# Attention sweep: value products one pair of steps later, key splits ahead of transposes, backward mLSTM in three steps

## The chip, the cores and the metric

The kernel runs on one core of one Trainium2 chip. The metric is the device time of one execution in microseconds (us). The core has five engines with a queue each: PE (matmuls and transposes, into PSUM banks), DVE (element-wise work), ACT (activation functions, casts and copies), POOL (element-wise work in SBUF) and SP, whose queue issues nearly all DMA transfers here. Each queue is worked off in order; engines wait for one another only through semaphores.

## The reference

One encoder layer over 2048 tokens of width 1024, in float32. Two groups of heads read one input projection, and their outputs are joined, projected, and followed by a feed-forward layer:

```python
h = rms_norm(x, g_mix_norm[l])
z = h @ w_in[l]
y_a = mlstm_group(q_m, k_m, v_m, o_m, gates, ...)   # 4 heads, forward + backward scan over chunks of 128
y_b = mla_group(c_q, c_kv, k_pe, cos, sin, ...)     # 4 heads, full softmax attention
x = x + jnp.concatenate([y_a, y_b], axis=-1) @ w_out[l]
h = rms_norm(x, g_ffn_norm[l])
x = x + jnp.square(jax.nn.relu(h @ w_ff1[l])) @ w_ff2[l]
```

In the attention group every block of queries is scored against all 2048 keys (128 + 64 values per key and query), a softmax is taken over the row, and the probabilities are multiplied with the values. In the mLSTM group a state matrix runs over the 16 chunks of 128 tokens in both directions; its gates (a cumulative sum of log-sigmoids and a running maximum) are needed before the first chunk.

## The kernel before

**Split products.** A float32 product is made of three passes: each operand is split into a high part (a cast on ACT, line 53, which rounds) and a low part (the difference, line 54, on DVE or POOL), and `mm3` (lines 69 to 71) adds high times high, low times high and high times low. So whatever comes to PE as a second operand first goes through a cast on ACT and a subtraction on DVE or POOL.

**The stages.** The input projection comes first (up to about 455 us of the trace), then the attention sweep with the mLSTM woven into it (about 455 to 1150 us), then the output projection and the feed-forward layer. From the attention sweep on the order of every queue is written out by hand: an instruction stands in its engine's queue where the program's text emits it.

**The attention sweep.** `attention` runs over 16 blocks `b` (4 heads of 4 blocks of 512 queries). A block has 16 steps `s`: for four groups `a` of 128 queries, four key tiles `j` of 512 keys. The global step is `g = 16 b + s`, and the loop takes the steps in pairs (`g0`, `g0 + 1`). The text of a pair is emitted in this order:

- two scores, five matmuls of 512 columns each, into one of three PSUM banks `ps`; behind each score stands DVE's copy with the row maximum (line 1092), which frees the bank;
- two chunks of value products, `pv`, three matmuls each (L69, L70, L71), which lag the scores by 20 steps. A chunk `(j, k)` reads column `k` of the transposed probabilities `pth` and `ptl` of key tile `j`, and each of them is written by the four transposes `a = 0..3` of that key tile;
- at one pair of a block `out`, DVE's product of the finished `pv` bank with the inverse row sums (line 1157);
- one step of the mLSTM generator (`next(work)`), here called the step in the middle of the pair;
- for each of the two steps: the exponential on ACT (line 1103) of probabilities scored four steps earlier, and `transpose_group`: four PE transposes of 128 columns (L1134) into one of two PSUM banks `ptp`, then cast to `pth` on ACT (line 53) and difference `ptl` on DVE (line 54). The transposes of block `b` come 16 steps behind its scores, the value products 20;
- a second step of the mLSTM generator at the end of the pair;
- then, at certain steps, loads and splits for what is to come: queries of the next block (`load_q`, `split_q`), keys of the next head (`load_k`, `split_k`: two casts on ACT and two differences), values (`load_v`, `split_v`).

Key tiles 1 to 3 of the next head are split in the last two pairs of a head, in steps `u = 4, 5, 6` of the last eight. Their buffers are those of the old head's tiles, which come free as its last scores are read.

**The mLSTM generator** gives up the word at each `yield`, and so decides only at which half pair its instructions stand. `mlstm_prelude` makes the gate tables: a chain of small operations, with PE transposes of `gs` (L662) and of `mr` (L673), between them eight short scans on DVE (L669), then tables `gn`, which the weights `kw` need. `mlstm_steps` then runs backward over chunks 15 to 1 in groups of two: per group one step with the outer products of the weighted keys `kw` and the values (PE, L759, one PSUM bank `pm` of two for each chunk), two steps in which DVE adds them to the running state (L768, L771) and the state is stored and the next values and keys are loaded, POOL weighing the next group's keys (L752) in the first of them, and one step with a load for the forward pass. After that it runs forward over 16 chunks of twelve steps each, whose `finish` has DVE's `num` (L893) and `sgt` (L904).

**The end of the sweep** is written out: after the last pair, the remaining value products of block 14 stand between the transposes of block 15 (`rest(n)` issues `n` chunks from the list `left`).

Of the kernel before, what the change touches and what calls it, by code (L numbers as in the profile page):

```python
# [25 lines left out]
NH = 4  # L26
# [578 lines left out]
def mlstm_prelude(c, psM):  # L605


    nc, tc = c.nc, c.tc
    H = P // 2
    with ExitStack() as st:  # L610
        pool = st.enter_context(tc.tile_pool(name="g_sb", bufs=1, reuse_waits="tile"))

        def bank():
            return psM.tile([P, 512], F32, name="pm")
# [42 lines left out]
        nc.vector.tensor_copy(gs[:, 1:2], cu[:, P - 1:P])  # L657
        yield
        yield
        pr = bank()[0:1, 0:256].rearrange("p (a t) -> p a t", a=2)  # L660
        for j in range(2):
            nc.tensor.transpose(pr[:, j, :], gs[:, j:j + 1], c.ident)  # L662
# [4 lines left out]
        for r in range(8):  # L667
            s = slice(r * NT, (r + 1) * NT - 1)
            nc.vector.tensor_tensor_scan(mr[:, r, 1:], g1[:, 1, s], g1[:, 0, s], 0.0, op0=ALU.max, op1=ALU.add)  # L669
        yield  # L670
        yield
        pm = bank()[:, 0:1]
# [62 lines left out]
def mlstm_steps(c, pool, ps, ld):  # L735


    nc = c.nc
# [176 lines left out]
    def weigh_all(n):  # L915
        for ch in groups[n]:
            kws[ch] = weigh(1, NT - 1 - ch, ld[ch][1])
# [3 lines left out]
    for n, grp in enumerate(groups):  # L921
        outs = [outer(kws.pop(ch), ld.pop(ch)[0]) for ch in grp]
        yield
        for k, ch in enumerate(grp):
            new = back[ch - 1] = advance(1, NT - 1 - ch, outs[k])
            if ch > 4:
                nc.sync.dma_start(c.d_C[ch - 1], new)
                ld[ch - 4] = mlstm_v(c, ch - 4), mlstm_k(c, ch - 4)
            if k == 0 and n + 1 < len(groups):
                weigh_all(n + 1)  # L930
            yield
        if 4 <= n < len(groups):
            loads[n - 4](0)
        yield
    for d in range(2):
        mask(0, d)

# [62 lines left out]
def attention(c, keep, drain, project):  # L1000

    nc, tc = c.nc, c.tc
    with ExitStack() as st:
# [42 lines left out]
        def load_v(h, j):  # L1046
            raw = vraw[h, j] = rp.tile([P, 512], F32, name="raw").rearrange("p (k d) -> p k d", k=4)
            nc.sync.dma_start(raw, c.d_va[j * 512:(j + 1) * 512, h * DV:(h + 1) * DV].rearrange(
                "(k p) d -> p k d", p=P))
# [49 lines left out]
        def softmax(b, a, j):  # L1099
            if (a, j) == (0, 0):  # L1100
                dens[b] = yp.tile([P, 4, 4], F32, name="rd4", bufs=2)
            p = probs[b, a, j]
            nc.scalar.activation(p, p, AF.Exp, bias=maxes[b, a], accum_out=dens[b][:, a, j:j + 1])  # L1103
# [85 lines left out]
        for g0 in range(0, 16 * N, 2):  # L1189
            pair = (g0, g0 + 1)  # L1190
            for g in pair:
                b, s = divmod(g, 16)
                score(b, *divmod(s, 4))
            for g in pair:
                bp, n = divmod(g - 20, 16)
                if bp >= 0:
                    pv(bp, *divmod(n, 4))
                    if n % 4 == 3:
                        next_v(bp, n // 4)
            if g0 % 16 == 2 and g0 > 32:  # L1200
                out(g0 // 16 - 2)()
            for g in pair:
                b, s = divmod(g, 16)
                h, i = divmod(g // 8, 2 * NB)
                u = g % 8
                if g == g0:
                    next(work, None)
                if g > 3:
                    r = g // 4 - 1
                    softmax(r // 4, r % 4, g % 4)  # L1210
                if g >= 16:
                    m = (g - 16) % 16
                    transpose_group(g // 16 - 1, *divmod(m, 4))
                if g > g0:
                    next(work, None)
                if s == 5 and b:
                    invert(b - 1)
                if s == 9 and b:
                    broadcast(b - 1)
                if b < N - 1:  # L1220
                    if s == 1:
                        load_q(*divmod(b + 1, NB))
                    if s == 7:
                        split_q(*divmod(b + 1, NB))
                if h < NH - 1:
                    if i == 2 and u == 1:
                        load_k(h + 1, 0)
                    if i == 4 and u == 1:
                        split_k(h + 1, 0)
                    if i == 6 and u in (4, 5, 6):  # L1230
                        load_k(h + 1, u - 3)
                    if i == 7 and u in (4, 5, 6):
                        split_k(h + 1, u - 3, nc.vector if u == 5 else nc.gpsimd)
                        if u == 6:
                            load_v(h + 1, 0)
                            load_v(h + 1, 1)
                if g in (6, 8, 10, 12):
                    split_v(0, g // 2 - 3)
                    if g < 10:
                        load_v(0, g // 2 - 1)  # L1240
            if g0 == 16 * N - 10:
                after = drain(rp)
                next(after)
        for _ in work:
            pass
        b = N - 1
        left = list(range(12, 16))

        def rest(n):
            for _ in range(n):  # L1250
# [5 lines left out]
        sl.close()  # L1256
        skq.close()
        next(after)
        rest(1)
        transpose_group(b, 0, 1)  # L1260
        softmax(b, 3, 2)
        rest(1)
# [5 lines left out]
        rest(1)  # L1268
        transpose_group(b, 1, 0, True)
        invert(b)  # L1270
        out(b - 1)()
        transpose_group(b, 1, 1)
        transpose_group(b, 1, 2, True)
# [1069 lines left out]
```

## Time and profile before

| | us |
|---|---|
| median of 3 runs (2561.45 to 2563.33) | 2562.35 |
| the profiled execution | 2561.93 |
| its span | 2560.1 |
| PE busy | 2532.7 |
| DVE busy | 1722.4 |
| ACT busy | 1294.7 |
| POOL busy | 376.9 |

Busy time is that of the span. PE's share is 99%, but its matmuls overlap: a matmul of 512 columns is drawn 0.39 us long and the next one starts 0.23 us after it, so busy PE is not PE at its peak, and a short wait may vanish under the drawn end of the matmul before. Waits are given with the engine that ended them; times of single instructions are read from the timeline, in us from the span's start.

### The profile page before, as it was taken

How to read it: one execution, taken by the hardware profiler on the slowest of the kernel's cores; microseconds unless marked ns; L12 is line 12 of the kernel's file. 1: busy time of each engine (PE TensorE's matmuls, PEld its weight loads, DVE VectorE, ACT ScalarE, POOL GpSimd, SP SyncE). 2: the span in 40 equal slices, each digit the busy share in tenths (PEclk: the TensorE clock that was granted, in tenths of full speed). 3: DMA queues.
4: the chain of work that ended last, by engine and by line, in shares of the span. 5: the costliest groups of instructions: out<-in, count | busy, mean ns of one | idle time of the engine just before them, and what ended most of it. 6: DMA issues, size and time to landing. Idle time of an engine off the chain costs nothing. (4 is left out here: it accounts for less than half of the span.)

```text
span 2560.1 us, 35765 instructions
## 1 busy us (share of the span) xinstructions
PE 2532.7 (99%) x12380; PEld 2111.7 (82%) x12380; DVE 1722.4 (67%) x3286; ACT 1294.7 (51%) x2900; POOL 376.9 (15%) x428
## 2 busy tenths in 40 slices
PE   9999999999999999999999999999999999999999
PEld 7888888787888887888888888888888888888887
DVE  5585467666666666678788787977775577666443
ACT  6455444656666676675445554655554323332332
POOL 1211121213223223200100000000000222322000
PEclk9999999999999999999999999999999999999999
DMA  5434234445353453335695555745447644444552
GB/s 176 144 116 144 94 115 143 107 131 112 88 114 109 98 125 95 73 103 189 206 297 191 197 196 191 253 152 167 145 146 278 220 146 147 146 143 145 214 181 95
DMA packets 295930, 392.53 MB, mean 153 GB/s; under 512 B 32261, under 2 KB 176964, under 8 KB 295748
## 3 DMA queue, kind: packets, MB, share of 16 engines
q1 hardware_dynamic: 293284, 385.78, 48.1%
q10 hardware_dynamic: 2464, 4.46, 0.5%
q8 instruction: 97, 1.59, 0.3%
q14 instruction: 85, 0.70, 0.1%
HBM read 258.51 MB, written 131.64 MB: 152 GB/s over the span
## 5 line engine op out<-in xcount | busy, mean ns | idle before, releaser
L69 PE MATMUL pd<-w2h,uh 128*128 128x512 f32 x896 | 348.7, 389 | 0.1
L70 PE MATMUL pd<-w2l,uh 128*128 128x512 f32 x896 | 348.6, 389 | 0.0
L71 PE MATMUL pd<-w2h,ul 128*128 128x512 f32 x896 | 348.5, 389 | 0.0
L54 DVE TENSOR_TENSOR ul<-ur,uh 128x1024 fp32r<-128x1024 f32 x110 | 153.7, 1397 | 252.8 <-ACT uh L53 252.7
L53 ACT CAST uh<-ur 128x1024 fp32r<-128x1024 f32 x110 | 116.0, 1055 | 395.5 <-PE pd L70 381.7
L54 DVE TENSOR_TENSOR ptl<-ptp,pth 128x512 fp32r<-128x512 f32 x248 | 171.2, 691 | 202.7 <-ACT pth L53 197.6
L53 ACT CAST pth<-ptp 128x512 fp32r<-128x512 f32 x248 | 143.6, 579 | 163.8 <-PE ptp L1134 162.9
L2011 DVE TENSOR_TENSOR e<-pu,e 128x512 f32<-128x512 f32 x224 | 151.3, 689 | 88.7 <-PE pu L71 87.7
L69 PEld LDWEIGHTS pd<-w2h,uh 128*128 128x128 f32 x896 | 168.2, 188 | 35.5 <-DVE e L2011 0.5
L71 PEld LDWEIGHTS pd<-w2h,ul 128*128 128x128 f32 x896 | 168.2, 188 | 34.9
L70 PEld LDWEIGHTS pd<-w2l,uh 128*128 128x128 f32 x896 | 168.2, 188 | 34.9
L1103 ACT ACTIVATE p<-p,nm 128x512 f32<-128x512 f32 x256 | 185.7, 725 | 0.0
L1092 DVE TENSOR_SCALAR_CACHE_REDUCE p<-ps 128x512 f32<-128x512 f32 x256 | 167.6, 682 | 20.4 <-PE ps L1091 20.3
L2175 POOL TENSOR_TENSOR r<-wr,r 128x512 f32<-128x512 f32 x48 | 78.0, 1624 | 623.9 <-DMA wr<-in_w 573.0
L69 PE MATMUL pz<-wh,hh 128*128 128x512 f32 (+1 forms) x384 | 149.7, 391 | 2.1 <-ACT hh L53 0.8
L71 PE MATMUL pz<-wh,hl 128*128 128x512 f32 (+1 forms) x384 | 150.1, 391 | 0.0
L70 PE MATMUL pz<-wl,hh 128*128 128x512 f32 (+1 forms) x384 | 149.2, 389 | 0.1
L2014 ACT ACTIVATE e<-e 128x512 f32<-128x512 f32 x128 | 80.9, 632 | 121.3 <-DVE e L2011 114.7
L1134 PE MATMUL ptp<-ident,p 128*128 128x128 f32 x992 | 130.3, 273 | 0.3 <-DVE ptl L54 0.3
L1134 PEld LDWEIGHTS ptp<-ident,p 128*128 128x128 f32 x992 | 113.9, 140 | 13.5 <-issue 1.4
L1087 PE MATMUL ps<-kh,qh 128*128 128x512 f32 x256 | 113.0, 441 | 1.7 <-ACT kh L53 1.1
L1879 ACT CAST r<-w1raw 128x512 fp32r<-128x512 f32 x104 | 64.5, 622 | 92.9 <-PE pu L71 92.2
(526 smaller groups left out, 6460.9 us busy)
## 6 DMA issues: line engine op xcount, KB each, us to landing
d_u<-e SPq DMA_DIRECT2D x224, 256.0 KB
ur<-d_u SPq DMA_DIRECT2D x110, 512.0 KB
wr<-in_w SPq DMA_DIRECT2D x96, 256.0 KB
w1raw<-in_w SPq DMA_DIRECT2D x42, 512.0 KB
raw<-in_w_in SPq DMA_DIRECT2D x48, 256.0 KB
r<-in_w SPq DMA_DIRECT2D x22, 512.0 KB
mb<-d_M SPq DMA_DIRECT2D x32, 256.0 KB
acc<-d_x SPq DMA_DIRECT2D x16, 512.0 KB
```

The lines of the kernel that those rows point to most:

```text
L53: r = nc.scalar.copy(hi, src)
L54: (eng or nc.vector).tensor_tensor(lo, src, hi.bitcast(F32), op=ALU.subtract)
L69: nc.tensor.matmul(out, ah, bh, start=first, stop=False, skip_group_check=more)
L70: nc.tensor.matmul(out, ah, bl, start=False, stop=False, skip_group_check=more)
L71: nc.tensor.matmul(out, al, bh, start=False, stop=last, skip_group_check=more)
L1087: nc.tensor.matmul(o, qh[:, qs], kh, start=True, stop=False)
L1092: nc.vector.tensor_scalar(p, o, SCALE, None, op0=ALU.mult, op1=ALU.max, accum_out=maxes[b, a][:, j:j + 1])
L1103: nc.scalar.activation(p, p, AF.Exp, bias=maxes[b, a], accum_out=dens[b][:, a, j:j + 1])
L1134: nc.tensor.transpose(pt[:, k, :], p[:, k * P:(k + 1) * P], c.ident)
L2011: nc.vector.tensor_tensor(out, o, t, op=ALU.add)
L2014: nc.scalar.activation(t, t, AF.Relu)
L2175: nc.gpsimd.tensor_tensor(R, wr, R, op=ALU.subtract)
```

## The change

No arithmetic changes, and each engine has the same instructions in another order. There are five parts, and the end of the sweep is adapted to the first.

- **Value products** lag the scores by 22 steps in place of 20, one pair more; `out` moves with them by a pair. At the end six chunks of block 14 are left in place of four: `rest(2)` stands first, and one more `rest(1)` ahead of `out`.
- **Key splits** of tiles 1 to 3 of the next head stand ahead of the transposes of their step, not behind them, and the tiles that are subtracted on POOL, DVE and POOL are now on POOL, POOL and DVE.
- **Query split** of the second block: at step 11 of the first block in place of 7 (the others stay).
- **Gate chain**: four more yields, two ahead of the transposes of `gs` and two ahead of the transposes of `mr`, so two half pairs each.
- **Backward chunks**: a group of two takes three steps in place of four; the load for the forward pass goes into the last of them. Over eight groups eight steps fall away, so that, with the four that the gate chain takes, the forward pass starts four half pairs earlier.

```diff
@@ mlstm_prelude
         nc.vector.tensor_copy(gs[:, 1:2], cu[:, P - 1:P])
         yield
         yield
+        yield
+        yield
         pr = bank()[0:1, 0:256].rearrange("p (a t) -> p a t", a=2)
...
+        yield
+        yield
         yield
         yield
         pm = bank()[:, 0:1]
@@ mlstm_steps, backward
             if k == 0 and n + 1 < len(groups):
                 weigh_all(n + 1)
+            if ch == grp[-1] and n >= 4:
+                loads[n - 4](0)
             yield
-        if 4 <= n < len(groups):
-            loads[n - 4](0)
-        yield
@@ attention, the loop over pairs
             for g in pair:
-                bp, n = divmod(g - 20, 16)
+                bp, n = divmod(g - 22, 16)
...
-            if g0 % 16 == 2 and g0 > 32:
+            if g0 % 16 == 4 and g0 > 32:
                 out(g0 // 16 - 2)()
...
                     softmax(r // 4, r % 4, g % 4)
+                if h < NH - 1 and i == 7 and u in (4, 5, 6):
+                    split_k(h + 1, u - 3, nc.vector if u == 6 else nc.gpsimd)
+                    if u == 6:
+                        load_v(h + 1, 0)
+                        load_v(h + 1, 1)
                 if g >= 16:
...
-                    if s == 7:
+                    if s == (7 if b else 11):
                         split_q(*divmod(b + 1, NB))
...
-                if i == 7 and u in (4, 5, 6):
-                    split_k(h + 1, u - 3, nc.vector if u == 5 else nc.gpsimd)
-                    if u == 6:
-                        load_v(h + 1, 0)
-                        load_v(h + 1, 1)
@@ attention, the end
-        left = list(range(12, 16))
+        left = list(range(10, 16))
...
-        rest(1)
+        rest(2)
         transpose_group(b, 0, 1)
...
         invert(b)
+        rest(1)
         out(b - 1)()
```

Where the order of the queues moves is shown at three places. Line numbers of the changed kernel are higher by three or four in these parts (L1134 is L1137 there, L759 is L763, L771 is L775, L1092 is L1095).

PE, at the end of the sweep, behind the last scores. `ptp` are the last transposes of block 14, `pm` the first of block 15, L69 to L71 the value products of block 14. Before:

```order
L1134 MATMUL ptp<-ident,p 128x128 x8
L1134 MATMUL pm<-ident,p 128x128 x4
L69 MATMUL pv<-pth,vh 128x512
L70 MATMUL pv<-ptl,vh 128x512
L71 MATMUL pv<-pth,vl 128x512
L1134 MATMUL ptp<-ident,p 128x128 x4
```

And now:

```order
L1137 MATMUL ptp<-ident,p 128x128 x8
L1137 MATMUL pm<-ident,p 128x128 x4
L69 MATMUL pv<-pth,vh 128x512
L70 MATMUL pv<-ptl,vh 128x512
L71 MATMUL pv<-pth,vl 128x512
L69 MATMUL pv<-pth,vh 128x512
L70 MATMUL pv<-ptl,vh 128x512
L71 MATMUL pv<-pth,vl 128x512
L1137 MATMUL ptp<-ident,p 128x128 x4
```

The value products stand one pair later against scores and transposes all through the sweep; here it is seen in two chunks more behind the last transposes. The first of them belong to key tile 2, whose transposes are two pairs back, where before they belonged to tile 3, transposed just ahead.

ACT, in the last two pairs of the first head. L1103 (now L1106) is the exponential, `pth` the cast of a transposed group, `kh` and `rh` the casts of one key tile of the next head, `num` a copy of the mLSTM. Before:

```order
L1103 ACTIVATE p,rd_6347<-p,nm 128x512
L53 CAST pth<-ptp 128x4x128
L53 CAST kh<-raw 128x512
L53 CAST rh<-raw 128x512
L1103 ACTIVATE p,rd_6347<-p,nm 128x512
L53 CAST pth<-ptp 128x4x128
L874 COPY num_6581<-pm 128x258
L53 CAST kh<-raw 128x512
L53 CAST rh<-raw 128x512
```

And now:

```order
L1106 ACTIVATE p,rd_6362<-p,nm 128x512
L53 CAST kh<-raw 128x512
L53 CAST rh<-raw 128x512
L53 CAST pth<-ptp 128x4x128
L1106 ACTIVATE p,rd_6362<-p,nm 128x512
L53 CAST kh<-raw 128x512
L53 CAST rh<-raw 128x512
L53 CAST pth<-ptp 128x4x128
```

The two casts of a key tile moved from behind the cast of the transposes to ahead of it, so each `pth` of these steps has two casts more in front of it.

DVE, in the backward chunks. L771 (now L775) adds an outer product to the state `C`, which frees its PSUM bank; L1092 (now L1095) are the copies of the two scores of a pair, `ptl` the differences of its two transposed groups. Before:

```order
L771 SCALAR_TENSOR_TENSOR C_5717<-C_5636,decb,pm 128x129 x2
L54 TENSOR_TENSOR ptl<-ptp,pth 128x4x128 x2
L771 SCALAR_TENSOR_TENSOR C_5743<-C_5717,decb,pm 128x129 x2
L1092 TENSOR_SCALAR p,mx<-ps 128x512 x2
L54 TENSOR_TENSOR ptl<-ptp,pth 128x4x128 x2
L1092 TENSOR_SCALAR p,mx<-ps 128x512 x2
L1096 TENSOR_REDUCE nm<-mx 128x1
L1157 TENSOR_TENSOR y<-pv,rb 128x512
L771 SCALAR_TENSOR_TENSOR C_5840<-C_5743,decb,pm 128x129 x2
```

And now:

```order
L775 SCALAR_TENSOR_TENSOR C_5768<-C_5711,decb,pm 128x129 x2
L1095 TENSOR_SCALAR p,mx<-ps 128x512 x2
L1099 TENSOR_REDUCE nm<-mx 128x1
L775 SCALAR_TENSOR_TENSOR C_5815<-C_5768,decb,pm 128x129 x2
L54 TENSOR_TENSOR ptl<-ptp,pth 128x4x128 x2
L1095 TENSOR_SCALAR p,mx<-ps 128x512 x2
L1160 TENSOR_TENSOR y<-pv,rb 128x512
L775 SCALAR_TENSOR_TENSOR C_5873<-C_5815,decb,pm 128x129 x2
```

The two additions of a group were followed by nearly a whole pair of other work (copies and differences); now those of the next group follow one half pair sooner. The outer products on PE stood at the end of every second pair; now they stand by turns at the end of a pair and in the middle of the next but one.

## The prediction

> **What bounds the kernel now.** I read the page's first part, then the waits of PE in the attention sweep, then the timeline around the longest of them.
>
> ```profile
> span 2560.1 us, 35765 instructions
> PE 2532.7 (99%) x12380; PEld 2111.7 (82%) x12380; DVE 1722.4 (67%) x3286; ACT 1294.7 (51%) x2900; POOL 376.9 (15%) x428
> ...
> PE pv L69 <- ACT pth L53: 4.8, 7, 1.0
> PE pv L70 <- DVE ptl L54: 3.4, 14, 0.4
> PE pm L673 <- DVE mr L669: 1.8, 1, 1.8
> PE ps L1087 <- ACT kh L53: 1.1, 1, 1.1
> PE pm L759 <- POOL kw L752: 0.8, 1, 0.8
> PE ps L1087 <- DVE p L1092: 0.7, 1, 0.7
> PE ptp L1134 <- DVE ptl L54: 0.3, 1, 0.3
> ```
>
> PE sets the time from end to end. An edit that adds no work and only moves it can win no more than what PE loses in waits, and the rows (waited-for engine, then us in total, times, longest) are all that it loses in the sweep but for 0.2 us: 12.9 us. Each part of the change is aimed at one or two of these rows. The listed figures are too small, though, since a wait is counted from the drawn end of the matmul before. One place shows by how much:
>
> ```profile
> 626.98 0.40 PE L1091 MATMUL ps<-rl,qr 128*128 128x512 f32 x1
> 628.21 0.50 PE L69 MATMUL pv<-pth,vh 128*128 128x512 f32 x1 [0.83 <-ACT pth L53]
> 628.93 0.50 PE L70 MATMUL pv<-ptl,vh 128*128 128x512 f32 x1 [0.23 <-DVE ptl L54]
> 629.27 0.39 PE L71 MATMUL pv<-pth,vl 128*128 128x512 f32 x1
> 629.50 0.39 PE L69 MATMUL pv<-pth,vh 128*128 128x512 f32 x1
> ```
>
> Undisturbed, matmuls start 0.23 us apart (629.27 to 629.50). From 626.98 to 629.27 are three intervals, 0.69 us, and it took 2.29: 1.60 lost, of which 1.06 is listed. Per L69 wait that is 1.23 - 0.23 - 0.83 = 0.17 unlisted; per L70 wait, from 628.21 to 629.27, 1.06 - 0.46 - 0.23 = 0.37.
>
> **The change part by part.**
>
> *Value products a pair later.* They wait because the fourth group of transposes that they read was transposed just ahead of the two scores in front of them. Now a whole pair more lies between, 16 matmuls of 512 columns at 0.23 us and 8 transposes, so 3.7 us and more against a longest lost time of 1.6. All 21 listed waits should go: 4.8 + 3.4 + 7 x 0.17 + 14 x 0.37 = **14.6 us**. The one in the tail (L69 behind the last transposes) is included; the two chunks that are moved into the tail, 6 x 0.23 = 1.4 us, fill that wait. Nothing is queued differently for the buffers: the cast that overwrites an old `pth` comes behind transposes that PE issues after the last products of it; the `pv` bank is freed by `out`, which moved along. I cost these at nothing, because PE's own order covers them.
>
> *Gate chain.* Between the transposes of `gs` and of `mr` stood ten score matmuls, 2.3 us; now twenty, 4.6 us, and eight transposes. The wait was not alone:
>
> ```profile
> 474.95 0.40 PE L1091 MATMUL ps<-rl,qr 128*128 128x512 f32 x1
> 477.10 0.19 PE L673 MATMUL pm<-ident,mr 1*128 1x1 f32 x1 [1.75 <-DVE mr L669]
> 477.83 0.63 PE L1089 MATMUL ps<-kh,ql 128*128 128x512 f32 x1
> 481.19 0.39 PE L1087 MATMUL ps<-kh,qh 128*128 128x512 f32 x1
> ...
> 474.60:477.90 3.30, 1.55 (x8) 0.95 (x7) 3.30 (x11) 3.30 (x9) 2.85 (x3) 0.97 0.00 0
> 477.90:481.40 3.50, 3.50 (x10) 2.75 (x9) 0.96 (x5) 3.03 (x9) 1.62 (x2) 0.54 0.00 0
> 481.40:484.80 3.40, 3.40 (x21) 2.93 (x20) 2.82 (x11) 1.83 (x7) 0.00 (x0) 1.00 0.03 3
> ```
>
> In the stage rows PE was busy 1.55 of 3.30 us, and in the next 3.5 us the granted clock (third figure from the end) was 0.54, then 1.00 again. Eight matmuls from 477.83 to 481.19 took 3.36 us, not 1.84: 1.5 lost. With the wait's 1.8 that is 3.3. The scans don't get shorter, however; they hold DVE, and so its copies of the scores:
>
> ```profile
> 474.02 0.40 DVE L665 COPY g<-pm 1x256 f32<-1x256 f32 x1
> 474.40 0.17 DVE L666 MEMSET mr<- 1x128 f32 x1
> 474.60 2.35 DVE L669 TENSOR_TENSOR_SCAN mr<-g 1x15 f32<-1x15 f32 x8
> 476.88 0.66 DVE L1092 TENSOR_SCALAR_CACHE_REDUCE p<-ps 128x512 f32<-128x512 f32 x1
> ```
>
> PE may run three banks ahead, three scores of 5 x 0.23 us = 3.5. Against that stand 0.40 + 0.17 ahead of the scans, 2.35 and 0.66 for the next copy = 3.6, and what the copy before them is late: I estimate 0.5 us of wait on `ps` in its place. Net **2.8**. The 0.7 on L1087 <- DVE earlier in the chain is untouched.
>
> By the Trainium skill (TensorE: Matmul & The Clock Gate, Part 1: The HAM clock gate) the clock halves after an idle window of about 3.4 us, for which 1.75 us of idleness is too short. The trace shows the half clock right behind a stretch that was idle for half of 3.3 us, so I take it to go with the wait; what follows otherwise is a rival below.
>
> *Backward chunks and `kw`.* The first outer product waited for POOL, which was busy with the query split; four half pairs later it is done with that. 0.8, and 0.17 unlisted as for an L69 wait, = **1.0**. Eight steps fewer cost and win nothing themselves, as PE has the same work in the sweep.
>
> *Key splits.* The wait on `kh` goes (1.1 and again 0.17 = **1.3**), since the casts are one transposed group sooner; the price is that transposes' casts come later. **0.3** on `ptp` I count with it.
>
> Gross: 14.6 + 2.8 + 1.0 + 1.3 + 0.3 = 20.0.
>
> *What comes back.* A wait of PE was also the time in which ACT and DVE caught up. Behind 628.2:
>
> ```profile
> 628.79 0.68 DVE L856 TENSOR_TENSOR mb<-pm,mb 128x512 f32<-128x512 f32 x1
> 629.39 2.68 DVE L893 SCALAR_TENSOR_TENSOR num<-num,rd,num 128x128 f32<-128x128 f32 x4
> 631.99 0.68 DVE L1092 TENSOR_SCALAR_CACHE_REDUCE p<-ps 128x512 f32<-128x512 f32 x1
> ...
> 632.77 0.48 PE L1087 MATMUL ps<-kh,qh 128*128 128x512 f32 x1
> ...
> 1125.14 1.13 DVE L893 SCALAR_TENSOR_TENSOR num<-num,rd,num 128x128 f32<-128x128 f32 x4
> ```
>
> Without 1.6 us of wait PE begins its next score at 631.2 and the second at 632.4, whose bank DVE frees at 632.7: 0.3 of 1.6 returns. The bounds are nothing (all waits end in slack) and the whole 14.6 (each moves to `ps` or `ptp`); I take a tenth, **1.5**, as this place is the nearest row. L893 took 2.68 us while POOL split the queries, 1.13 when POOL was idle. The Trainium skill (SBUF — State Buffer, SBUF: two separate sides) calls the port that the two share an exclusive lock, and the change sets two key splits in a row on POOL; this is one way to the first rival.
>
> At the three head changes each `pth` has casts of 0.62 us in front, two per split:
>
> ```profile
> 952.18 0.62 ACT L53 CAST kh<-raw 128x512 fp32r<-128x512 f32 x1
> 952.70 0.62 ACT L53 CAST rh<-raw 128x512 fp32r<-128x512 f32 x1
> ```
>
> 1.2 to 2.5 us of delay per pair against the 3.7 us that scores and products give before the next transposes need the bank; bounds 0 and 2.5 at each of three, I take 0.7: **2.1**. For the outer products in mid pair I add **0.3**.
>
> Net 20.0 - 3.9 = 16.1. The profiled execution took 2561.93 us (1.8 more than its span, which no part touches), so 2545.8; the median of the runs lies 0.4 above it: **2546.2 us**.
>
> **The rivals.**
>
> *The waits move.* ACT and DVE stay as late as they were and PE meets them at the `ptp` and `ps` banks. If half of the 14.6 returns, half of the three small terms (2.6) too, and the head changes cost 1.1 each, the gain is 7.3 + 2.8 + 1.3 - 3.3 = 8.1: 2554. For it: DVE's 2.68. Against: in the longest stretch
>
> ```profile
> 585.00:1010.00 425.00, 416.75 (x2374) 349.35 (x2373) 278.57 (x709) 291.91 (x831) 131.20 (x135) 1.00 0.43 107
> ```
>
> DVE works 66% and ACT 69% of the time, so each makes up about 1.5 us in a pair of 4.6 (10.3 us for two, with 1.1 of outer products, in the rows of the last rival).
>
> *The clock drop isn't the wait's.* By that page's rule the half rate has another cause, falls on the same stretch of matmuls, and 1.5 us stay: 2547.7. Against it: the one low stretch of the sweep stands right behind its longest wait.
>
> *Nothing moves.* The engines that feed PE set the pace: at 66 and 69% unlikely; then 2561.
>
> *Slower, at the backward groups.* They begin 10.3 us apart, two pairs, and shall begin one and a half apart, 7.7 us:
>
> ```profile
> 514.18 1.10 PE L759 MATMUL pm<-v,kw 128*64 128x129 f32 x16
> 524.50 1.10 PE L759 MATMUL pm<-v,kw 128*64 128x129 f32 x16
> ...
> 514.80 0.57 SPq L731 DMA_DIRECT2D knat<-d_k  x1
> ...
> 518.00 0.62 POOL L752 TENSOR_TENSOR kw<-knat,gn 128x256 f32<-128x256 f32 x1 [2.38 <-DMA knat<-d_k]
> ```
>
> If store, loads and weighing set that distance, PE waits 2.6 us in each of seven groups, longer than the wait that went with the half clock, so 1.5 more each: 7 x 4.1 = 28.7 against 16.1, 2575. It decides once keys are weighed later than the outer products want them. They were loaded at 514.80, weighed by 518.62 and wanted at 524.50, 5.9 us later; 2.6 of that go, and 3.3 remain.
>
> **How the numbers follow.** Forecast 61%, the waits move 17%, the clock rule 10%, nothing moves 8%, slower 4%. The forecast's own bounds are no return (20.0: 2542.4) and all returns doubled (2550); the first rival ends at 2554. The range 2541 to 2555 leaves out the last two cases. About 0.2%, 5 us, is what a measurement of this kernel can tell from no change: faster 0.88, same 0.08, slower 0.04.
>
> **What would show it.** In the changed kernel the waits of `pv` are gone from PE's list, and `ps` and `ptp` rows, if they grow, hold less than 4 us. The transposes of `mr` follow without a wait, and no stage of the sweep is granted half the clock. The forecast is wrong if `ptp` or `ps` waits on ACT and DVE sum to 8 us or more, or if L763 waits for `kw` or the state.

## The result, and the profile after

The changed kernel took 2544.25 us (median of four runs, 2542.08 to 2544.83) against 2562.84 for the kernel before beside it: a ratio of 0.9926 with a 95% interval of 0.9909 to 0.9943. Its profiled execution took 2542.08 us, 19.9 less than that of before. The forecast was 2546.2 us, range 2541 to 2555.

The page's first part in the changed kernel, where PE is busy 9.0 us less than before and its span 19.8 us shorter:

```profile
span 2540.3 us, 35812 instructions
PE 2523.7 (99%) x12380; PEld 2111.3 (83%) x12380; DVE 1726.1 (68%) x3286; ACT 1293.7 (51%) x2900; POOL 380.7 (15%) x428
```

The whole list of PE's waits between 455 and 1140 us there (engine, waited-for line, then us in total, times, longest):

```profile
PE ps L1090 <- DVE p L1095: 2.4, 4, 1.3
PE ptp L1137 <- DVE ptl L54: 0.3, 1, 0.3
PE ps L1155 <- ACT pth L53: 0.2, 1, 0.2
```

The rows on `pv`, `kh`, `mr` and `kw` are gone. What is left on `ps` has one large part, which was not there before; it stands in the gate chain, as PE's timeline shows:

```profile
478.22 0.50 PE L1093 MATMUL ps<-rh,qr 128*128 128x512 f32 x1
478.56 0.40 PE L1094 MATMUL ps<-rl,qr 128*128 128x512 f32 x1
480.30 0.50 PE L1090 MATMUL ps<-kh,qh 128*128 128x512 f32 x1 [1.34 <-DVE p L1095]
...
482.53 0.22 PE L677 MATMUL pm<-ident,mr 1*128 1x1 f32 x1
```

From 478.56 to 480.30 are 1.74 us where 0.23 would do: 1.5 lost. The transposes of `mr` (482.53) follow without a wait, and the stretches that held the half clock before now have the full one (third figure from the end):

```profile
474.60:477.90 3.30, 3.30 (x17) 2.52 (x15) 2.94 (x10) 3.30 (x10) 3.22 (x3) 1.00 0.69 170
477.90:481.40 3.50, 2.08 (x9) 1.23 (x8) 3.40 (x11) 1.61 (x5) 1.55 (x2) 1.00 0.00 0
```

Where did the time come from? One program's stages can be measured by the starts of PE's matmuls. From the last one of the input projection to the first of the output projection, in the timelines of before and after:

```profile
457.77 0.39 PE L71 MATMUL pz<-wh,hl 128*128 128x512 f32 x1
1156.58 0.47 PE L69 MATMUL po<-B11h,r 128*128 128x512 f32 x1
```

```profile
457.74 0.39 PE L71 MATMUL pz<-wh,hl 128*128 128x512 f32 x1
1138.10 0.48 PE L69 MATMUL po<-B11h,r 128*128 128x512 f32 x1
```

That stretch, here called *the sweep*, shrank from 698.8 to 680.4 us, by 18.4; the other 1.4 us fell in the output projection and the first part of the feed-forward layer (0.62 and 0.76), which no part touches. In the profiles of all kernels below, the last matmul of the input projection, the same code in each, started between 457.2 and 460.0 us. So parts of one or two us are compared by the length of the sweep, and even that differed by 0.8 us between two profiles of the changed kernel (680.4, and 681.2 in the last experiment).

Each ratio is to the kernel before that ran beside it, whose median lay between 2562.38 and 2563.71 us.

| kernel | median us | ratio to before, 95% | sweep us |
|---|---|---|---|
| before | 2562.84 | | 698.8 |
| value products alone | 2546.42 | 0.9936, 0.9921 to 0.9951 | 683.8 |
| gate chain alone | 2560.56 | 0.9991, 0.9981 to 1.0 | 695.9 |
| key splits alone | 2562.13 | 0.9998, 0.9988 to 1.0007 | 698.2 |
| backward chunks alone | 2564.22 | 1.0005, 0.9995 to 1.0014 | 700.9 |
| the change | 2544.25 | 0.9926, 0.9909 to 0.9943 | 680.4 |
| the change without key splits | 2544.32 | 0.9929, 0.9917 to 0.9942 | 680.0 |
| the change without backward chunks | 2545.39 | 0.9932, 0.9918 to 0.9946 | 681.6 |
| the change, query split at 7 | 2544.56 | 0.993, 0.9917 to 0.9942 | 680.5 |
| that, scans in halves | 2545.26 | 0.9932, 0.992 to 0.9945 | 681.6 |
| the change, POOL relieved | 2544.88 | 0.9931, 0.9917 to 0.9944 | 680.2 |
| that, loads ahead | 2542.85 | 0.9923, 0.9909 to 0.9936 | 679.0 |
| that, query split at 9 | 2542.19 | 0.9923, 0.991 to 0.9937 | 677.9 |
| the change again, beside the last | 2545.12 | 0.9931, 0.9919 to 0.9944 | 681.2 |

### The profile page after: what moved, and what is told of

Read it like the earlier page. It is cut to its first block, busy times and chain, and to the rows that moved or that the text cites. A ratio compares the mean times of both kernels' runs of the same rounds, so it can differ in the third digit from the quotient of the medians.

```text
span 2540.3 us, 35812 instructions
## 1 busy us (share of the span) xinstructions
PE 2523.7 (99%) x12380; PEld 2111.3 (83%) x12380; DVE 1726.1 (68%) x3286; ACT 1293.7 (51%) x2900; POOL 380.7 (15%) x428
## 5 line engine op out<-in xcount | busy, mean ns | idle before, releaser
L69 PE MATMUL pd<-w2h,uh 128*128 128x512 f32 x896 | 348.8, 389 | 0.1
L71 PE MATMUL pd<-w2h,ul 128*128 128x512 f32 x896 | 348.7, 389 | 0.0
L69 PEld LDWEIGHTS pd<-w2h,uh 128*128 128x128 f32 x896 | 168.2, 188 | 35.4 <-DVE e L2015 0.5
L71 PEld LDWEIGHTS pd<-w2h,ul 128*128 128x128 f32 x896 | 168.2, 188 | 34.9
L1106 ACT ACTIVATE p<-p,nm 128x512 f32<-128x512 f32 x256 | 185.8, 726 | 2.6 <-DVE nm L1099 2.6
L1095 DVE TENSOR_SCALAR_CACHE_REDUCE p<-ps 128x512 f32<-128x512 f32 x256 | 167.4, 682 | 15.2 <-PE ps L1094 15.1
L69 PE MATMUL pz<-wh,hh 128*128 128x512 f32 (+1 forms) x384 | 149.5, 391 | 1.7 <-ACT vo L495 0.7
L71 PE MATMUL pz<-wh,hl 128*128 128x512 f32 (+1 forms) x384 | 150.0, 391 | 0.0
L1137 PE MATMUL ptp<-ident,p 128*128 128x128 f32 x992 | 130.6, 274 | 0.5 <-DVE ptl L54 0.3
L1137 PEld LDWEIGHTS ptp<-ident,p 128*128 128x128 f32 x992 | 113.6, 140 | 14.1 <-issue 1.4
L1090 PE MATMUL ps<-kh,qh 128*128 128x512 f32 x256 | 112.8, 441 | 2.4 <-DVE p L1095 2.4
```

The source lines that it names most:

```text
L69: nc.tensor.matmul(out, ah, bh, start=first, stop=False, skip_group_check=more)
L71: nc.tensor.matmul(out, al, bh, start=False, stop=last, skip_group_check=more)
L1090: nc.tensor.matmul(o, qh[:, qs], kh, start=True, stop=False)
L1095: nc.vector.tensor_scalar(p, o, SCALE, None, op0=ALU.mult, op1=ALU.max, accum_out=maxes[b, a][:, j:j + 1])
L1137: nc.tensor.transpose(pt[:, k, :], p[:, k * P:(k + 1) * P], c.ident)
```

## The experiments

**Each part alone.** The theory: each part removes its own wait, and the value products bring nearly all. The rival: the waits move to `ps` and `ptp`.

*Value products alone* (labels of the kernel before, L1087 for L1090 and so on):

```diff
-                bp, n = divmod(g - 20, 16)
+                bp, n = divmod(g - 22, 16)
...
-            if g0 % 16 == 2 and g0 > 32:
+            if g0 % 16 == 4 and g0 > 32:
...
-        left = list(range(12, 16))
+        left = list(range(10, 16))
```

> The kernel before with only the value products (and out, and the end of the sweep) one pair later. My theory: all waits of pv on pth and ptl go, about 1.5 us come back on ps or ptp, the waits on mr (1.8, with the half clock), kh (1.1) and kw (0.8) stay as they were: 13 us less, 2549 +- 1.5. The rival (waits move): at least half comes back on ps and ptp unless the key splits and the gate chain are changed too, 2555 or more. A second rival (the parts only work together): under 4 us gained.

Measured: 2546.42 us, better than expected. Its list of PE's waits, without the last two rows (0.3 and 0.2):

```profile
PE pm L673 <- DVE mr L669: 2.4, 1, 2.4
PE ps L1087 <- ACT kh L53: 1.0, 1, 1.0
PE ps L1087 <- DVE p L1092: 0.8, 1, 0.8
PE pm L759 <- POOL kw L752: 0.8, 1, 0.8
...
```

All 21 waits of `pv` are gone and no row grew in their place but that on `mr`. Behind the first transposes of the sweep the stage is 15.8 us shorter (673.1 to 657.3), while the first block, from the input projection to the first transposes, lost 0.8 to the longer wait on `mr`. So the rival fell here: in the list nothing of this term returned.

*Gate chain alone* (the four yields; the query split stays at 7):

```diff
         yield
         yield
+        yield
+        yield
         pr = bank()[0:1, 0:256].rearrange("p (a t) -> p a t", a=2)
...
             nc.vector.tensor_tensor_scan(mr[:, r, 1:], ...)
+        yield
+        yield
```

> The kernel before with only the four yields in the gate chain (the query split stays at step 7). My theory: the wait on mr goes and the half clock with it, the scans take 2.35 us as before (in the changed kernel they took 3.45) and leave about 0.5 us of wait on ps, kw has no wait: 3.8 us less, 2558.8 +- 1.5, where the later mLSTM may shift pv waits by 1. If the clock drop isn't the wait's: half clock in the same stretch, 2560.3.

Measured: 2560.56 us, outside the 2558.8 +- 1.5 that was expected and near the 2560.3 of the rival. The rival's half clock isn't there, though: no wait on `mr`, no half clock, 0.56 us on `ps` behind the scans, and the first block is 3.2 us shorter (25.7 to 22.5). That difference is rough. Up to the first transposes the kernel before and those with value products, key splits and backward chunks alone have the same order of work, and took 25.7, 26.5, 26.6 and 23.8 us there, the last without a half clock. Behind the first block the kernel is 0.3 us longer, although the wait on `kw` (0.8) is gone: the forward chunks now end four half pairs later, among the written-out end of the sweep, and the list shows what that costs:

```profile
PE ps L1156 <- ACT pth L53: 0.9, 1, 0.9
PE pm L1138 <- DVE ptl L54: 0.7, 1, 0.7
```

*Key splits alone* and *backward chunks alone*:

```diff
+                if h < NH - 1 and i == 7 and u in (4, 5, 6):
+                    split_k(h + 1, u - 3, nc.vector if u == 6 else nc.gpsimd)
...
-                    if i == 7 and u in (4, 5, 6):
-                        split_k(h + 1, u - 3, nc.vector if u == 5 else nc.gpsimd)
```

> The kernel before with only the key splits (and the value loads behind them) ahead of the transposes, on POOL, POOL, DVE. My theory: the 1.1 us wait on kh goes, but the casts of pth behind it are later and pv still reads them right away, so the pv waits at the three head changes grow by up to 1.2 each: between 1.3 less and 2.3 more, 2562.9 +- 1.5. The rival, that this part wins for itself: 2561 or less with no larger pv wait.

```diff
+            if ch == grp[-1] and n >= 4:
+                loads[n - 4](0)
             yield
-        if 4 <= n < len(groups):
-            loads[n - 4](0)
-        yield
```

> The kernel before with only the backward chunks in three steps (the forward pass eight half pairs earlier). My theory: no time is won or lost, 2562.4 +- 1.5; outer products wait only once, for the first kw (0.8). The rival (loads or the state set the distance of the groups): waits of L759 on kw or C of 2.6 us in seven groups and half clock behind them, up to 2591.

In the whole time neither won anything that could be told from the spread. With the keys first, the wait on `kh` goes, and at that head change the casts in front of `pth` make one value product, still one pair early, wait 1.9 us; all waits on `pth` are 6.3 us (4.8 before), those on `ptl` 2.7 (3.4 before):

```profile
PE pv L69 <- ACT pth L53: 6.3, 6, 1.9
PE pv L70 <- DVE ptl L54: 2.7, 12, 0.3
PE pm L673 <- DVE mr L669: 2.6, 1, 2.6
```

The sweep of this kernel is 0.6 us shorter than before: 0.9 longer in the first block, which this part doesn't touch, and 1.5 shorter behind it. By that the part was worth a little by itself, where the rows on the value products alone would say that it lost.

With the backward chunks alone the slower rival's mechanism shows itself, once, against the expectation that only the first `kw` is waited for. PE's row, and POOL's beside it:

```profile
549.54 1.13 PE L759 MATMUL pm<-v,kw 128*64 128x129 f32 x8 [2.80 <-POOL kw L752]
...
548.87 0.62 POOL L752 TENSOR_TENSOR kw<-knat,gn 128x256 f32<-128x256 f32 x1 [8.59 <-DMA knat<-d_k]
```

The keys came late, the outer product waited 2.8 us for them, and half the clock followed at once. The sweep is 2.1 us longer than before: 4.0 longer behind the first block, and 1.9 shorter in it, where a wait of 2.4 us on `mr` cost no half clock this time.

**One part taken back.**

*Without the key part*:

```diff
-                if h < NH - 1 and i == 7 and u in (4, 5, 6):
-                    split_k(h + 1, u - 3, nc.vector if u == 6 else nc.gpsimd)
...
+                    if i == 7 and u in (4, 5, 6):
+                        split_k(h + 1, u - 3, nc.vector if u == 5 else nc.gpsimd)
```

> The changed kernel without its key part: the splits of the next head's tiles 1 to 3 stand behind the transposes again. Theory: that part is worth nothing by itself once the value products are later: the wait on kh comes back (1.0 to 1.3 us), the small waits on ps and ptp at the three head changes (0.4 + 0.8 + 0.3 us) go, so within 0.5 us of the changed kernel (2542.1 profiled). Rival, the prediction's own sum: the kh wait of 1.3 us comes back and 2.1 us of casts ahead of the transposes go, 0.8 us faster. Other rival: the casts behind the transposes now meet the products of a pair later, pv waits come back at the head changes, 2 us slower.

Measured: sweep 680.0, no difference. By the distances of matmul starts the wait on `kh` at the second head change costs 1.2 us here; in the change the second and third head changes cost 0.39, 0.30, 0.49 and 0.32, together 1.5, on `ps` and `ptp`, and these are gone here. The part exchanges one for the other.

*Without the backward part*:

```diff
-            if ch == grp[-1] and n >= 4:
-                loads[n - 4](0)
             yield
+        if 4 <= n < len(groups):
+            loads[n - 4](0)
+        yield
```

> The changed kernel without its backward part: groups of two chunks in four steps again. Theory: the three steps pay only for the four yields of the gate chain; without them the forward chunks end four half pairs later than in the kernel before and run into the end of the sweep, where PE then waits on casts and differences as in the kernel with the gate chain alone (1.1 + 0.7 us there), so 1.5 to 2 us slower than the changed kernel, 2543.6 to 2544.1 profiled; the keys are weighed with over 2 us of slack. Rival: the groups' closer distance costs PE something that its list of waits doesn't show, and with four steps the time is the same or less.

Measured: sweep 681.6, with 1.2 us on `ptl` and 0.8 on `pth` listed in the tail. Against the first profile of the change that is 1.2 us more, against the second 0.4. The waits are those expected; that the time is longer can't be told from the spread.

*Query split back at step 7*:

```diff
-                    if s == (7 if b else 11):
+                    if s == 7:
```

> The changed kernel with one part undone: the query split of the second block back at step 7. My theory: the eight scans took 3.45 us in place of 2.35 because the two differences of the query split ran on POOL beside them, and that is why the wait on ps in the gate chain was 1.5 us and not the 0.5 that I predicted. Then here the scans take about 2.35 us, the wait is about 0.5 us, and the profiled execution is about 1.0 us below that of the changed kernel (2542.1), so 2541.0. Rival: the scans are long for another reason (the transposes and copies of more steps between): scans 3.45 us, wait 1.5 us, no change in time. Second rival: the split at 7 delays something else in the first block (the weighing of keys on POOL, or a score's copy), and a wait of 0.8 us or more takes the place.

This theory fell. The scans took 3.10 us and the wait on `ps` stayed at 1.5, sweep 680.5. POOL was busy beside the scans all the same, now with the first head's values:

```profile
478.51 3.10 DVE L671 TENSOR_TENSOR_SCAN mr<-g 1x15 f32<-1x15 f32 x8
...
477.45 1.29 POOL L1077 TENSOR_TENSOR qr<-raw,qr 64x512 fp32r<-64x512 f32 x1
478.82 2.67 POOL L54 TENSOR_TENSOR vl<-raw,vh 128x512 fp32r<-128x512 f32 x2
```

*Scans in halves*:

```diff
         for r in range(8):
             ...
-        yield
-        yield
-        yield
-        yield
+            if r in (3, 7):
+                yield
+                yield
...
-                    if s == (7 if b else 11):
+                    if s == 7:
```

> The changed kernel with the query split back at step 7 and the eight scans emitted in two halves of four, each with two of the four yields behind it, so that a score's copy can stand between them on DVE. Theory: the wait on ps comes from DVE held by the scans for longer than three banks cover; halves of 1.2 us leave none, so the whole 1.5 us of wait in the chain goes and the profiled execution is 2540.6. Rival: DVE is late by its sum of work and not by the block of scans; then the wait stays between 0.3 and 0.5 us and nothing is won over the kernel with only the split moved.

The wait on `ps` behind the scans went, but PE then met ACT, which had worked without a pause: 0.84 and 0.69 us were lost at the next transposes, as much as was won, and 0.95 at the outer products. (PE's list names the difference `ptl` on DVE there; DVE itself had waited 2.14 us for ACT's cast `pth`.) Here "the waits move" was true. DVE's two halves say more:

```profile
477.77 1.67 DVE L671 TENSOR_TENSOR_SCAN mr<-g 1x15 f32<-1x15 f32 x4
...
481.19 0.42 DVE L671 TENSOR_TENSOR_SCAN mr<-g 1x15 f32<-1x15 f32 x4
```

Four scans of the same shape take 1.67 us beside a POOL that is busy (478.10 to 481.05, one pause of 0.36) and 0.42 while it is idle (481.05 to 481.69). In the change, three operations of POOL lie beside the eight scans:

```profile
475.50 1.30 POOL L54 TENSOR_TENSOR ql<-raw,qh 128x512 fp32r<-128x512 f32 x1
476.87 1.30 POOL L1077 TENSOR_TENSOR qr<-raw,qr 64x512 fp32r<-64x512 f32 x1
478.25 1.28 POOL L54 TENSOR_TENSOR vl<-raw,vh 128x512 fp32r<-128x512 f32 x1
...
476.20 3.45 DVE L671 TENSOR_TENSOR_SCAN mr<-g 1x15 f32<-1x15 f32 x8
```

**POOL kept out of the way.** The new theory: an operation of DVE that reads SBUF twice and meets one of POOL waits until that one is over.

```diff
+        load_q(0, 1)
         load_v(0, 0)
...
-                    if s == 1:
+                    if s == 1 and b:
                         load_q(*divmod(b + 1, NB))
-                    if s == (7 if b else 11):
+                    if s == 7:
...
-                if g in (6, 8, 10, 12):
-                    split_v(0, g // 2 - 3)
-                    if g < 10:
-                        load_v(0, g // 2 - 1)
+                if g in (18, 22, 26, 30):
+                    split_v(0, (g - 18) // 4)
+                    if g < 26:
+                        load_v(0, (g - 10) // 4)
```

> The changed kernel with POOL and ACT relieved while the gate chain runs: the queries of the second block are loaded ahead of the sweep and split at step 7, and the values of the first head are split at steps 18, 22, 26, 30 in place of 6, 8, 10, 12. Theory: an operation of DVE that reads two SBUF tiles and meets one of POOL waits for the whole of it. With POOL idle the eight scans take 0.9 to 1.2 us in place of 3.45, and f (L650, 1.27 us beside a value split) about 0.3; so both waits on ps in the chain go, 0.85 + 1.51 us. As ACT has five casts less there and doesn't wait for the queries' load, it isn't late at the transposes behind, and the first block and the sweep together take 2.3 us less than the changed kernel's 680.4. Rival one: ACT stays late and PE meets it at ptp, as with the scans in halves: 680.4 to 681.3. Rival two: the keys of a backward group come no sooner while PE does, and about 1 us is lost at the outer products (L763 <- kw): 679.0. If the scans still take 3 us, the theory of the port is wrong.

The scans took 0.76 us, less even than the 0.9 to 1.2 expected, and `f` 0.29, and there was no wait behind them. But the query split now met two other operations of the chain, earlier:

```profile
471.62 1.02 DVE L654 TENSOR_TENSOR u<-li,b 128x128 f32<-128x128 f32 x1
472.68 1.46 DVE L655 TENSOR_TENSOR_SCAN cu<-u 128x128 f32<-128x128 f32 x1
...
471.21 1.29 POOL L54 TENSOR_TENSOR ql<-raw,qh 128x512 fp32r<-128x512 f32 x1 [15.84 <-ACT qh L53]
472.58 1.28 POOL L1077 TENSOR_TENSOR qr<-raw,qr 64x512 fp32r<-64x512 f32 x1
```

`ql` ends at 472.50 and `u` at 472.64; `qr` ends at 473.86 and `cu` at 474.14. Elsewhere these two take 0.29 and 0.43 us. So 1.76 us of DVE went, a wait on `ps` of 1.44 stood there, and the sweep was 680.2: the time was the rival's, by a mechanism that only the theory had.

*The loads ahead*, on top of it:

```diff
+            if ch > 4:
+                kn = mlstm_k(c, ch - 4)
+                ld[ch - 4] = mlstm_v(c, ch - 4), kn
             new = back[ch - 1] = advance(1, NT - 1 - ch, outs[k])
             if ch > 4:
                 nc.sync.dma_start(c.d_C[ch - 1], new)
-                ld[ch - 4] = mlstm_v(c, ch - 4), mlstm_k(c, ch - 4)
```

> The kernel with POOL and ACT relieved, and in the backward groups the loads of the next values and keys stand ahead of DVE's additions and of the store of the state, keys first. Theory: what decides the outer products' wait is when the keys are loaded; with the loads about 1 us sooner the wait on kw is gone, and first block and sweep together take 678.0 us (about 1 us less than without it, if that kernel waits there; the same if it doesn't). Rival: the keys take 6 to 9 us to land whenever they are issued, since the transfers ahead of them in the queue set it; then the wait stays as it is.

The keys for the outer products at 549.6 were weighed by 547.08, and no wait on `kw` is left (0.2 us listed without this part). The sweep is 679.0, where 678.0 was expected. Of the 1.2 us less than without this part, 0.5 lie behind the first block, where the loads stand; the other 0.8 lie in the first block, which it doesn't touch.

```profile
546.46 0.62 POOL L756 TENSOR_TENSOR kw<-knat,gn 128x256 f32<-128x256 f32 x1 [0.44 <-DMA knat<-d_k]
```

*Query split at step 9*, on top of both, and *the change again* on the same chip:

```diff
-                    if s == 7:
+                    if s == (7 if b else 9):
```

> The kernel with POOL and ACT relieved and the loads ahead, and its query split at step 9 in place of 7. At 7 the two differences on POOL met u (L654, 0.29 us alone, 1.02 there) and the scan behind it (L655, 0.42 alone, 1.46 there), which cost a wait on ps of 1.25 us. Theory of the port: POOL's 2.6 us fit between those operations of the gate chain and the eight scans, where DVE only copies scores; u takes 0.29, the scan 0.42, the eight scans 0.8, and no wait on ps over 0.4 us is left in the chain. First block and sweep together 677.7 us, 2.7 below the changed kernel's 680.4. Rival: the split meets the eight scans, or the casts of the queries make ACT late, and 1 us or more of wait on ps or ptp stays: 678.7 or more.

> The changed kernel itself, on the same chip as the quiet one, so that the two are compared directly: 680.4 us for first block and sweep together as in its first profile, with 0.3 us of spread; the median 2 to 3 us above the quiet one's if the waits of the gate chain are what differs, and no more than 1 us if they come back elsewhere.

Now POOL's two operations lie where DVE copies scores out of PSUM, and every operation of the chain has its short time:

```profile
471.54 0.29 DVE L654 TENSOR_TENSOR u<-li,b 128x128 f32<-128x128 f32 x1
471.87 0.43 DVE L655 TENSOR_TENSOR_SCAN cu<-u 128x128 f32<-128x128 f32 x1
...
476.02 0.76 DVE L671 TENSOR_TENSOR_SCAN mr<-g 1x15 f32<-1x15 f32 x8
...
472.55 1.30 POOL L54 TENSOR_TENSOR ql<-raw,qh 128x512 fp32r<-128x512 f32 x1 [17.07 <-ACT qh L53]
473.93 1.29 POOL L1079 TENSOR_TENSOR qr<-raw,qr 64x512 fp32r<-64x512 f32 x1
```

The sweep takes 677.9 us (677.7 expected), with one distance 0.20 us too long in the whole gate chain. The median is 2542.19 us (2541.03 to 2544.96) against 2545.12 (2543.75 to 2546.09) for the change beside it, 2.9 us less, and four of its five runs lie below the fastest of the change. Against before their intervals overlap, so as a ratio of times the gain is likely rather than settled; in the sweep's length it is 2.5 and 3.3 us against the two profiles of the change.

The second profile of the change has waits that its first one hadn't: on the queries, whose split at step 11 comes just as PE wants them (1.12 and 0.32 us lost), and on `kw` (0.71). The first of these stand in place of the 1.5 us behind the scans: the first block takes 23.8 and 23.9 us in the two profiles. A wait of L763 on `kw` is one of the things that the prediction named as showing it wrong; its price here is 0.7 us.

```profile
PE ps L1093 <- POOL qr L1077: 0.9, 1, 0.9
PE pm L763 <- POOL kw L756: 0.6, 1, 0.6
```

## Why the prediction was right, and where not

**What bounds the kernel** held: PE's waits were the whole stock, and the sweep became shorter by 18.4 us of the 20.0 that I had counted as gross. Net I had 16.1. Two parts bring nearly all of it: value products and gate chain alone shorten the sweep by 15.0 and 2.9 us. It is luck that the products brought 1.2 us more than their term and the gate chain 1.0 less than its own; what is left of the error is the return, priced too high.

**Value products: 14.6, of which 1.5 to return.** Alone 15.8 came, and no row grew in its place. Two sizes were off. The unlisted part of 14 + 7 waits was scaled up from one place (0.37 and 0.17), and was at least 1.2 us too small in all. And the tenth that I let return, from one place where DVE was 0.3 us behind, left no row in the list.

**Gate chain: 2.8.** Alone it brought 3.2 in the first block, with 0.56 us on `ps` where I said 0.5. In the change it brought 1.9. The step that failed is "2.35 for the scans", which I took for their length. It was the length that they happened to have: 0.76 us of work and the rest of a POOL operation or two. In the kernel before, where they ran from 474.60, these were

```profile
473.94 1.29 POOL L1074 TENSOR_TENSOR qr<-raw,qr 64x512 fp32r<-64x512 f32 x1
475.31 1.27 POOL L54 TENSOR_TENSOR vl<-raw,vh 128x512 fp32r<-128x512 f32 x1
```

In the change they met three and took 3.45, and `ps` waited 1.5. The move of the query split, which decides what POOL does beside them, I had not costed at all; undoing it alone showed that it wasn't the cause either, since the value splits then stand there.

**`kw`: 1.0.** It came, but the step "3.3 us remain" failed. The groups alternate between 9.4 and 6.6 us apart; for the one at 550.39 the keys were issued at 541.95 and the second of them was weighed from 549.66 to 550.28:

```profile
549.66 0.62 POOL L756 TENSOR_TENSOR kw<-knat,gn 128x256 f32<-128x256 f32 x1 [0.27 <-DMA knat<-d_k]
...
550.39 1.10 PE L763 MATMUL pm<-v,kw 128*64 128x129 f32 x16
```

0.1 us was left, and in the second profile of the change it was missed by 0.7. I had taken one group's load for the duration of all. So the slower rival's mechanism, to which I gave 4%, was real; what was wrong with it is its price, seven times 4.1 us, where it struck once.

**Key splits: 1.3 won, 2.1 returned.** 1.2 and 1.5 were measured. Right in kind, and 0.6 us too high in the return; beside the others the part makes no difference that the sweep shows.

**Backward chunks cost and win nothing themselves.** Alone they lost 2.1 us of the sweep. In the change they give back the four half pairs that the gate chain takes, and with them the tail's waits (1.2 and 0.8 us listed without them, 0.2 with them). By these waits the two parts belong together, which I had not seen; in the length of the sweep it isn't shown.

**What comes back: 3.9.** Measured 1.5 at the head changes, and nothing for the outer products in mid pair or in the tail (the 0.2 us listed there stood in the kernel before as well). With the 1.0 more on `ps` in the chain and the 1.2 more on `pv`, 20.0 + 1.2 - 1.0 - 1.5 = 18.7, against the sweep's 18.4; the 0.3 left over is less than the 0.8 between two profiles of the change.

**The clock rule** as a rival fell: in every kernel whose chain has no long wait, that stretch of matmuls had the full clock. But whether a wait costs the half clock depends on more than its length, as the last section shows.

## What to carry to other kernels

Price a part of a change within the whole, and not by its own wait alone: the key splits gained a little by themselves and nothing beside the later value products, and the backward chunks lost time alone and made no clear difference in the change. A duration in a profile is that of the operation among its neighbours; before it goes into a sum, look for the same form elsewhere in the trace, and where one of the same shape is several times shorter, ask what runs beside it. To see a change of one us in 2500, compare the stage that it touches, by the starts of its first and last matmul, and not the whole run.

## What the runs showed of the hardware

**POOL can stop DVE for a whole operation.** Eight scans of one partition and 15 elements took between 0.76 and 3.45 us, and `u`, a difference of 128x128, between 0.29 and 1.02, by what POOL did beside them; the operations that were held ended 0.03 to 0.3 us behind the end of POOL's operation of 1.3 us. Copies of scores, which read PSUM, took 0.63 to 0.69 us either way. The Trainium skill (SBUF — State Buffer, SBUF: two separate sides) states it so: an operation of DVE with two SBUF inputs and one of POOL that reads SBUF exclude each other for the length of the instruction. The traces agree, and they add that smallness is no protection, since a scan of 0.1 us waits as long as a large one. By these rows engines wait for one another not only through semaphores, and such a wait is drawn as busy time of DVE, not as a wait. I had cited the rule for L893 and not asked where else it holds.

**The half clock goes by windows.** Each half-clock stretch within the sweep lasted 3.413 us. If time is cut into windows of that length so that one begins where the half clock does, the windows just ahead of it had little PE work. PE busy is the second figure behind the colon. The kernel before, then those with value products and key splits alone:

```profile
474.31:477.72 3.41, 1.66 (x8) 1.10 (x7) 3.38 (x13) 3.41 (x11) 2.96 (x3) 1.00 0.00 0
475.76:479.17 3.41, 1.00 (x5) 0.62 (x4) 3.41 (x8) 3.41 (x11) 3.10 (x3) 1.00 0.00 0
476.35:479.76 3.41, 0.85 (x4) 0.43 (x4) 3.41 (x11) 3.41 (x9) 3.01 (x4) 1.00 0.00 0
```

The kernel with backward chunks alone, at its wait on `mr`, and then ahead of and within its half clock:

```profile
474.23:477.64 3.41, 2.34 (x11) 1.58 (x9) 3.34 (x13) 1.92 (x5) 1.61 (x2) 1.00 0.84 206
477.64:481.05 3.41, 2.10 (x10) 1.78 (x11) 2.89 (x8) 3.41 (x10) 3.10 (x3) 1.00 0.00 0
545.91:549.32 3.41, 0.83 (x10) 0.42 (x8) 0.42 (x2) 0.00 (x0) 0.45 (x1) 1.00 0.52 61
549.32:552.73 3.41, 3.19 (x17) 2.83 (x18) 0.30 (x1) 0.92 (x2) 3.25 (x4) 0.50 0.97 281
```

The four windows ahead of a half clock are 49, 29, 25 and 24% busy. The wait of 2.4 us on `mr` in the last kernel fell across two windows, which stayed 69 and 62% busy (2.34 and 2.10 of 3.41), and cost no clock. The least busy window that kept the full clock behind it, in the profiles of all these kernels, had 50%; it lies in the input projection of the change with POOL relieved and loads ahead:

```profile
71.20:74.61 3.41, 1.69 (x12) 1.19 (x10) 3.41 (x14) 0.63 (x1) 0.52 (x1) 1.00 0.00 0
74.61:78.03 3.42, 3.42 (x18) 2.74 (x15) 3.35 (x15) 0.97 (x2) 0.00 (x0) 1.00 0.48 150
```

So a wait of some 1.75 to 2.5 us may or may not cost another 1.5, by where it falls. The Trainium skill (TensorE: Matmul & The Clock Gate, Part 1: The HAM clock gate) has the free-running window of this length; that it must be idle is not what these traces show, since half idle was enough. By these windows the limit lies near half; as the ends of matmuls are modelled, 49 and 50% are too close to place it.

The granted clock that is on record for every execution shows the same of the kernel before. Of its 52 executions beside the experiments 13 have 1.000; a stretch of 3.413 us at half rate would make 0.999 of it. Their median is 2561.0 us, that of the other 39 is 2563.6. All ten executions with the gate chain alone have 1.000, with a median of 2560.6. So most of what that part won in the median seems to be the half clock, which the kernel before doesn't pay in every execution.
